# Modulation strips of a two-layer diffusion step: their matmuls beside the projections, one or two row chunks at a time or four

## The chip, the cores and the metric

The kernel runs on one core of a Trainium2 chip. The metric is the time of one execution on the device, in microseconds (us). The engines are PE (matrix products), DVE (vector operations), ACT (scalar operations, activations), POOL (GpSimd, here conv additions and memsets) and SP, which issues most DMA transfers. Each engine works through its own instructions in order and waits on semaphores for the others. SBUF is the memory on the chip that the engines read and write; PSUM, in banks, is where PE puts its results.

## The reference

Two layers work on 1152 tokens: 1024 latent tokens and 128 context tokens, each with 1024 features. What matters here is how the modulation enters:

```python
def ada_modulate(x, cond, norm_g, w_ada, b_ada):
    m = jax.nn.silu(cond) @ w_ada + b_ada
    shift, scale, gate = jnp.split(m, 3, axis=-1)
    h = rms_norm(x, norm_g) * (1.0 + scale[:, None, :]) + shift[:, None, :]
    return h, gate[:, None, :]
```

`cond` is one row for the context and one for the latent tokens, so `silu(cond) @ w_ada` is a product of 2 rows by a matrix of 1024 x 3072 for each layer. Layer 0 then projects `h` into the parts a, b, ga, q, k, v and gb. `a * sigmoid(b)` goes through a depthwise convolution of width 31, a layer norm and a SiLU, and is gated by `silu(ga)`; q, k and v go through an attention over a clamped 8 x 16 neighbourhood and all context keys, gated by `silu(gb)`. Both halves are concatenated and multiplied by `w_out`. Layer 1 projects its `h` into u and g, pools u over windows of 2, 4, 8 and 16 tokens, and multiplies by its own `w_out`. Each layer's result is multiplied by its gate and added to its input. The outputs are both streams after both layers, and the context keys and values of layer 0.

## The kernel before

**Tiling.** Tokens stand in three groups of 384. Matrices of float32 are split into a high and a low part, and a product is the sum of three matmuls of such parts. A chain of 24 matmuls (8 row blocks of 128, three products each) fills one PSUM bank: in L230 with 384 tokens as columns, for a, b, ga, gb and the projections of layer 1; in L237 with 128 tokens by 256 features, for v, q and k, where two chains share a bank, 48 matmuls in a row.

**Stages.** The rows of shift and scale of layer 0 come first, from the `wada` tiles. Then come items of work, one for each piece of `w_in_0`: `p_ab` for c = 0 to 3 (a and b of one quarter of the conv features each, three token groups g, two chains for each), `p_v` twice, `p_qk` four times, then gb and ga, the attention, the output of layer 0, and layer 1. The stretch of `p_ab`, `p_v` and the start of `p_qk` is 75 to 240 us in the profile.

**The strips.** What else of the modulation is needed, the gate of layer 0 and shift, scale and gate of layer 1, is computed beside these items, in three strips (`ada_strips`, called in `ada_rest`): for layer 0 four pieces of 256 columns, for layer 1 twice four pieces of 384. A strip has eight row chunks. Each chunk is one transfer (`wad`, 512 KB or 768 KB) by `dma_later` (L264, on SP's queue) into one of six slots `ADS`, and four matmuls (L360) with 2 columns of the two conditions as weights; the four go to the rows 0, 32, 64 and 96 of the bank through `tile_position`. Each such matmul of float32 is two records in the profile, so a chunk is eight. The bank (`tp`, of which there are two) is summed over the eight chunks.

**What follows a strip.** `fin` of the first strip is `ada_gate`: rows of the bias come by DMA (`gb`, L411), DVE adds and scales (L412, L413), and the result goes to memory (`gsc`, L414). `fin` of the others is `ada_cols`: POOL sets a tile `adr` to zero (L382) and DVE copies four pairs of rows into it (L384). It returns `ada_turn`, which is the strip's turn: three transposes on PE (L390) and additions on DVE (L278, L279). For the last strip the gate is formed as well.

**Who sets the order.** Steps stand in the queue `adq`, nine for a strip: eight chunks and the turn. `ada_steps(n)` takes n of them. It is called behind the chains of each token group in `p_ab` (two steps, one for c = 0), behind each pair of token blocks in `p_v` (one step), and before the first item of `p_qk`, where all that is left is taken. Between them `bg` advances streams of work in the background: the convolution, where for a tap ACT multiplies (L551) and POOL adds (L553) or DVE does both (L564). The first chains and the attention are put in order by hand; elsewhere the framework's scheduler puts each engine's instructions in order, from its own estimate of times, so that an edit of one step can move others. Of the last `qk` step DVE multiplies by `rstd` (L729), which POOL computes (L113, L114).

Of the kernel before, what the change touches and what calls it, by code (L numbers as in the profile page):

```python
# [46 lines left out]
def _body(tc, nc, A, O, const, wp, arena, tmpp, smp, psp):  # L47
# [7 lines left out]
    def slot(i, dtype=F32, name="s"):  # L55
        return arena.tile([P, SLOT], dtype, tag=f"S{i}", bufs=1, name=nm(name))
# [4 lines left out]
    def tmp(name="t"):  # L61
        return tmpp.tile([P, 512], F32, tag="t", name=nm(name))
# [22 lines left out]
    for w in (2, 4, 8, 16):  # L85
        t = const.tile([P, w], F32, name=f"corr{w}")
# [259 lines left out]
    adq = deque()  # L346

    def ada_strips(l, col, n, fin):

        st = {}  # L350

        def step(k):
            w = slot(ADS[st_i[0] % len(ADS)], name="wad")[:, : 4 * n]
            st_i[0] += 1
            dma_later(w, A[f"w_ada_{l}"][k * P : (k + 1) * P, col : col + 4 * n])
            if k == 0:
                st["b"] = bank("tp")
            for q in range(4):
                r = 32 * q
                te.matmul(  # L360
                    st["b"][r : r + 2, :n], sc[:, k, :], w[:, q * n : (q + 1) * n],
                    start=(k == 0), stop=(k == 7), tile_position=(0, r),
                )
            if k == 7:
                st["then"] = fin(st["b"])

        for k in range(8):
            adq.append(lambda k=k: step(k))
        adq.append(lambda: st["then"] and st["then"]())

    st_i = [0]

    def ada_steps(n=None):
        while adq and n != 0:
            adq.popleft()()
            n = None if n is None else n - 1

    def ada_cols(l, b, c0):

# [37 lines left out]
    def ada_rest():  # L417
        def fin11(b):
            then = ada_cols(1, b, 12)
            ada_gate(1, b, G, 1, P)  # L420
            return then

        ada_strips(0, 2 * D, 256, lambda b: ada_gate(0, b, 256, 0, 0))
        ada_strips(1, 0, G, lambda b: ada_cols(1, b, 0))
        ada_strips(1, 4 * G, G, fin11)

    def load_gates(l):
        gt = {}
# [217 lines left out]
    def p_ab(c):  # L646
        def glu(c, g, pa_, pb_):
            if g == 0:
                ut[c] = slot(US[c], name="u")[:, :UW] if c < 3 else gr[:, :UW]
                gp.memset(ut[c][:, 0:15], 0.0)  # L650
                gp.memset(ut[c][:, 1039:1054], 0.0)
                gp.memset(ut[c][:, 1182:1197], 0.0)
            th = tmp("th")
            se.activation(th[:, :G], pb_[:, :G], AF.Tanh, scale=0.5)
            for a, n, d in ((0, G, 15 + g * G),) if g < 2 else ((0, 256, 15 + 768), (256, P, 1054)):
                ve.scalar_tensor_tensor(ut[c][:, d : d + n], th[:, a : a + n], 1.0, pa_[:, a : a + n], ALU.add, ALU.mult)
            ready[c] = g + 1

        def chains(x, g, W):
            pa_, pb_ = bank("mm"), bank("mm")  # L660
            chain_ws(pa_[:, :G], W, 0, h0, g)
            chain_ws(pb_[:, :G], W, P, h0, g)
            glu(x, g, pa_, pb_)

        def fn(W):
            if c == 0:
                E = mybir.EngineType
                with tc.manual_schedule(engines={E.PE, E.Activation, E.DVE}):
                    bs = first_chains()
                units.update({x: [first_w[x, 0], first_w[x, 1]] for x in range(2)})  # L670
                W = units[0]
                late_vectors()
                for x, g in bs:
                    glu(x, g, *bs[x, g])
                make_h0(2)
                chains(1, 1, units[1])
            for g in range(2 if c < 2 else 0, 3):
                chains(c, g, W)
                bg(6000)
                ada_steps(2 if c else 1)  # L680
        return fn

    def p_v(vb):
        def fn(W):
            for t in range(0, 9, 2):
                b = bank("mm")
                n = min(2, 9 - t)
                for i in range(n):
                    chain_tok(b[:, i * 256 : (i + 1) * 256], W, h0, t + i)
                if t == 8:  # L690
                    se.copy(VP[:, vb * 256 : (vb + 1) * 256], b[:, :256])
                else:
                    s = tmp("vst")
                    se.copy(s, b)  # L694
                    se.dma_start(
                        vs[t * P : (t + 2) * P, vb * 256 : (vb + 1) * 256].rearrange("(a p) c -> p a c", p=P),
                        s.rearrange("p (a c) -> p a c", a=2),
                    )
                bg(4500)
                ada_steps(1)  # L700
            if vb == 1:
                se.dma_start(O[3][0], VP.rearrange("p (h d) -> p h d", d=64))
        return fn
# [4 lines left out]

    def p_qk(pr):
        def fn(W):  # L710
            if pr == 0:
                ada_steps()
            if pr == 2:
                bg_until(lambda: len(done) >= 1)
            for t in range(0, 9, 2):
                n = min(2, 9 - t)
# [757 lines left out]
```

## Time and profile before

| | |
|---|---|
| time, median of 3 runs | 974.99 us (974.53 to 975.31) |
| the profiled execution | 977.55 us, span 975.8 us |
| PE busy | 948.4 us, 97% of the span |
| DVE busy | 601.9 us, 62% |
| ACT busy | 404.4 us, 41% |
| POOL busy | 369.8 us, 38% |
| granted clock of PE, mean | 0.996 |

The span reaches from the first to the last instruction of the profiled execution; its own time is that of the whole execution. Busy shares are means over all stages. Records of PE overlap, since a matmul begins before the one ahead of it has ended; distances between starts are what counts. The granted clock is a share of PE's full clock.

### The profile page before, as it was taken

What the parts mean: (1) busy time and instruction counts of PE and PEld (TensorE: products, weight loads), DVE (VectorE), ACT (ScalarE), POOL (GpSimd) and SP (SyncE); (2) the same over time, 40 slices, a digit from 0 to 9 for tenths busy, and PEclk for the clock granted to TensorE, in tenths of its full rate; (3) what the DMA queues carried; (4) which work ended last, traced back from release to release, by engine and by line L of the source; (5) the groups of instructions that cost most, each with busy time, mean ns of one, the idle gap of its engine ahead of it and who ended that gap; (6) DMA issues with size and microseconds to landing.
All of it is one profiled execution on the core that took longest, in us unless ns stands there. A gap on an engine that the chain in (4) does not pass through costs nothing.

```text
span 975.8 us, 16659 instructions
## 1 busy us (share of the span) xinstructions
PE 948.4 (97%) x6388; PEld 866.3 (89%) x6388; DVE 601.9 (62%) x1243; ACT 404.4 (41%) x815; POOL 369.8 (38%) x485
## 2 busy tenths in 40 slices
PE   4999999899999999999999999999999999999998
PEld 2899888789999999987887888889999999998887
DVE  3658999989783444457778447666335554585332
ACT  4374676765411244238887223344222122231010
POOL 2354899889943201024456145430000000004231
PEclk9999999899999999999999999999999999999999
DMA  9946955525111111135335412251111111133211
GB/s 311 304 190 153 348 183 184 173 88 185 46 47 46 48 44 44 36 90 142 109 114 175 130 65 108 84 165 44 34 43 33 44 44 55 65 112 129 105 65 66
DMA packets 87531, 108.54 MB, mean 111 GB/s; under 512 B 10700, under 2 KB 73036, under 8 KB 87339
## 3 DMA queue, kind: packets, MB, share of 16 engines
q1 hardware_dynamic: 82539, 95.93, 30.9%
q0 software_dynamic: 2576, 9.18, 2.4%
q10 hardware_dynamic: 2336, 2.36, 0.7%
q8 instruction: 50, 0.82, 0.3%
q14 instruction: 30, 0.25, 0.1%
HBM read 94.64 MB, written 21.57 MB: 119 GB/s over the span
## 4 chain that ended last, share of the span: by engine, by line
PE 82%; POOL 5%; DVE 3%; DMA 3%; ACT 2%; issue 2%; SPq 1%; DVEq 0%; ACTq 0%; POOLq 0%
PE mm L230 33%; PE mm L237 15%; PE mm L1210 10%; PE mm L1203 10%; POOL zc L553 5%; PE cv L985 3%; PE tp L976 2%; PE mm L952 2%; PE mm L1373 2%; DVE cv L564 1%; DMA x<-in_x_sample 1%; DMA raw<-in_w_in 1%; PE tp L443 1%; SPq L212 1%; PE cv L230 1%
## 5 line engine op out<-in xcount | busy, mean ns | idle before, releaser
L230 PE MATMUL mm<-h,whi 128*128 128x384 f32 x1504 | 389.5, 339 | 1.0 <-POOL h L450 0.4
L230 PEld LDWEIGHTS mm<-h,whi 128*128 128x128 f32 x1504 | 271.6, 189 | 6.8 <-issue 2.0
L230 PE MATMUL mm<-h,wlo 128*128 128x384 f32 x752 | 252.8, 337 | 0.0
L553 POOL TENSOR_TENSOR zc<-zc,gr 128x384 f32<-128x384 f32 x138 | 148.5, 1078 | 32.7 <-ACT gr L551 24.5
L237 PE MATMUL mm<-whi,h 128*128 128x256 f32 x864 | 160.6, 287 | 0.0
L237 PEld LDWEIGHTS mm<-whi,h 128*128 128x128 f32 x864 | 137.4, 194 | 6.5 <-ACT vst L694 3.3
L230 PEld LDWEIGHTS mm<-h,wlo 128*128 128x128 f32 x752 | 141.9, 189 | 0.0
L237 PE MATMUL mm<-wlo,h 128*128 128x256 f32 x432 | 123.3, 285 | 0.0
L187 DVE TENSOR_TENSOR wlo<-raw,whi 128x1024 fp32r<-128x1024 f32 (+1 forms) x56 | 67.5, 1206 | 53.3 <-ACT whi L186 53.2
L564 DVE SCALAR_TENSOR_TENSOR cv<-u,convw,cv 128x384 f32<-128x384 f32 (+1 forms) x208 | 95.8, 514 | 1.3
L1210 PE MATMUL mm<-wrh,zs 128*128 128x512 f32 x288 | 92.4, 392 | 0.2 <-POOL wrh L1179 0.2
L1203 PE MATMUL mm<-whi,zs 128*128 128x512 f32 (+1 forms) x304 | 92.5, 379 | 0.0
L186 ACT CAST whi<-raw 128x1024 fp32r<-128x1024 f32 (+1 forms) x56 | 56.9, 1018 | 69.8 <-PE mm L230 25.9
L237 PEld LDWEIGHTS mm<-wlo,h 128*128 128x128 f32 x432 | 84.0, 194 | 0.0
L1217 POOL TENSOR_TENSOR y<-y,og 128x512 f32<-128x512 f32 x34 | 48.6, 1430 | 83.4 <-DVE og L1215 80.3
L551 ACT ACTIVATE gr<-u,convw 128x384 f32<-128x384 f32 (+2 forms) x128 | 64.3, 531 | 30.5 <-POOL zc L553 29.8
L970 POOL TENSOR_SCALAR p<-p,st 128x512 f32<-128x512 f32 x64 | 48.6, 773 | 47.6 <-DVE st L968 31.7
L1203 PEld LDWEIGHTS mm<-whi,zs 128*128 128x128 f32 x304 | 56.0, 188 | 10.6 <-ACT whi L186 0.2
L1210 PEld LDWEIGHTS mm<-wrh,zs 128*128 128x128 f32 x288 | 53.9, 188 | 11.8 <-POOL wrh L1179 0.6
L1215 DVE TENSOR_TENSOR og<-mm,gr 128x512 f32<-128x512 f32 x34 | 23.3, 687 | 59.3 <-PE mm L1210 35.0
L533 ACT ACTIVATE th<-mm 128x384 f32<-128x384 f32 x48 | 23.5, 489 | 81.7 <-PE mm L230 81.5
L1203 PE MATMUL mm<-wlo,zs 128*128 128x512 f32 (+1 forms) x152 | 57.2, 378 | 0.0
(215 smaller groups left out, 1393.2 us busy)
## 6 DMA issues: line engine op xcount, KB each, us to landing
raw<-in_w_in SPq DMA_DIRECT2D x28, 512.0 KB
wad<-in_w_ada SPq DMA_DIRECT2D x16, 768.0 KB
wada<-in_w_ada SPq DMA_DIRECT2D x16, 512.0 KB
raw<-in_w_in SPq DMA_DIRECT2D x32, 256.0 KB
raw<-in_w_out SPq DMA_DIRECT2D x16, 512.0 KB
y0scr<-y POOLq DMA_DIRECT2D x9, 512.0 KB, 3.2
y<-y0scr SPq DMA_DIRECT2D x9, 512.0 KB
x<-in_x_sample SPq DMA_DIRECT2D x8, 512.0 KB
```

Source lines behind the costliest of these rows:

```text
L186: se.copy(hi[:, :n], raw[:, :n])
L187: ve.tensor_tensor(lo[:, :n], raw[:, :n], f(hi[:, :n]), ALU.subtract)
L230: te.matmul(out, wsl(units, a, k, c0, P), hsl(hs, b, k, g), start=(k == 0 and i == 0), stop=(k == nk - 1 and i == 2))
L237: te.matmul(out, hsl(hs, p, k, g, a, P), wsl(units, q, k, 0, 256), start=(k == 0 and i == 0), stop=(k == 7 and i == 2))
L551: se.activation(pr[:, o : o + n], src, AF.Copy, scale=w)
L553: gp.tensor_tensor(z, z, pr, ALU.add)
L564: ve.scalar_tensor_tensor(zp if k == 30 else acc, src, convw[:, c, k : k + 1], zp if k == NPTS[c] else acc, ALU.mult, ALU.add)
L970: gp.tensor_scalar(ps[i][:, e, :], ps[i][:, e, :], st[:, 4 + e : 5 + e], 0.0, ALU.mult, ALU.add)
L985: te.matmul(ob[64 * e : 64 * e + 64, i * P : (i + 1) * P], vw[j0 + i][x][:, 64 * e : 64 * e + 64], pts[i][:, e, n * P : (n + 1) * P], star ...
L1203: te.matmul(b[:, c0 : c0 + n], zs[p][:, k, :], WL[k // 2][q][:, k % 2, c0 : c0 + n], start=(k == 0 and i == 0), stop=(k == 7 and i == 2))
L1210: te.matmul(b, zs[p][:, k, :], WR[q][k // 3][:, k % 3, :], start=(k == 0 and i == 0), stop=(k == 7 and i == 2))
L1217: gp.tensor_tensor(yv, yv, t, ALU.add)
```

## The change

An entry of the queue is now a list of steps, called a portion here: four chunks of a strip. The turn of a strip is no entry of its own; it stands at the head of the next strip's first portion (`owed_turn`), and that of the last strip in a portion alone. `ada_steps` takes one portion, and is called at seven named places: behind the token groups (c, g) = (1, 2), (2, 1), (3, 0) and (3, 2) of `p_ab`, and behind the blocks (vb, t) = (0, 4), (1, 0) and (1, 6) of `p_v`. The call in `p_qk` is gone. The instructions are the same on each engine, in another order.

```diff
--- before.py
+++ after.py
@@ -364,16 +364,17 @@
             if k == 7:
                 st["then"] = fin(st["b"])
 
-        for k in range(8):
-            adq.append(lambda k=k: step(k))
-        adq.append(lambda: st["then"] and st["then"]())
-
-    st_i = [0]
-
-    def ada_steps(n=None):
-        while adq and n != 0:
-            adq.popleft()()
-            n = None if n is None else n - 1
+
+        then, owed_turn[:] = list(owed_turn), [lambda: st["then"] and st["then"]()]
+        adq.append(then + [lambda k=k: step(k) for k in range(4)])
+        adq.append([lambda k=k: step(k) for k in range(4, 8)])
+
+    st_i, owed_turn = [0], []
+
+    def ada_steps(n=1):
+        for _ in range(min(n, len(adq))):
+            for step in adq.popleft():
+                step()
 
     def ada_cols(l, b, c0):
 
@@ -423,6 +424,7 @@
         ada_strips(0, 2 * D, 256, lambda b: ada_gate(0, b, 256, 0, 0))
         ada_strips(1, 0, G, lambda b: ada_cols(1, b, 0))
         ada_strips(1, 4 * G, G, fin11)
+        adq.append(list(owed_turn))
 
     def load_gates(l):
         gt = {}
@@ -677,7 +679,8 @@
             for g in range(2 if c < 2 else 0, 3):
                 chains(c, g, W)
                 bg(6000)
-                ada_steps(2 if c else 1)
+                if (c, g) in ((1, 2), (2, 1), (3, 0), (3, 2)):
+                    ada_steps()
         return fn
 
     def p_v(vb):
@@ -697,7 +700,8 @@
                         s.rearrange("p (a c) -> p a c", a=2),
                     )
                 bg(4500)
-                ada_steps(1)
+                if (vb, t) in ((0, 4), (1, 0), (1, 6)):
+                    ada_steps()
             if vb == 1:
                 se.dma_start(O[3][0], VP.rearrange("p (h d) -> p h d", d=64))
         return fn
@@ -708,8 +712,6 @@
 
     def p_qk(pr):
         def fn(W):
-            if pr == 0:
-                ada_steps()
             if pr == 2:
                 bg_until(lambda: len(done) >= 1)
             for t in range(0, 9, 2):
```

On PE, in the order of before, the 24 chunks stand in 18 groups between chains: in the first strip groups of a quarter of a chunk, three quarters, 2, 2, 2 and 1; in the second 2, 2, 2, 1 and 1; in the third six of 1 and one of 2. Of the changed kernel they stand in six groups of four. The next rows are PE's order of before at the first group of two (`tp_996` is the bank of the first strip, `mm` banks are those of the chains, a row with x4 is one chunk).

```order
L230 MATMUL mm_1030<-h_756,whi_568 128x384
L230 MATMUL mm_1030<-h_755,wlo_569 128x384
L360 MATMUL tp_996<-wad_1095,sc 2x256 x4
L360 MATMUL tp_996<-wad_1101,sc 2x256 x4
L230 MATMUL mm_1119<-h_249,whi_1007 128x384
L230 MATMUL mm_1119<-h_250,whi_1007 128x384
```

In the changed kernel the same place has four chunks, and no chunk stands earlier (`tp_1090` is now the bank of the first strip).

```order
L230 MATMUL mm_1023<-h_756,whi_568 128x384
L230 MATMUL mm_1023<-h_755,wlo_569 128x384
L360 MATMUL tp_1090<-wad_1088,sc 2x256 x4
L360 MATMUL tp_1090<-wad_1095,sc 2x256 x4
L360 MATMUL tp_1090<-wad_1101,sc 2x256 x4
L360 MATMUL tp_1090<-wad_1107,sc 2x256 x4
L230 MATMUL mm_1125<-h_249,whi_1000 128x384
L230 MATMUL mm_1125<-h_250,whi_1000 128x384
```

What moved: the first chunk's four matmuls, which were parted over two earlier places, and the fourth chunk, which came a token group later.

The second place is the order on DVE around the copies into `adr` of the second strip (its bank is `tp_1519` in both). Before, they are rows 253 to 256 of DVE's order; the products that form the conv input (L656, `gr`) stand some thirty rows ahead.

```order
L564 SCALAR_TENSOR_TENSOR cv_2084<-u_1169,convw,cv_2084 128x384
L564 SCALAR_TENSOR_TENSOR cv_1893<-u_743,convw,cv_1893 128x128
L564 SCALAR_TENSOR_TENSOR cv_2084<-u_1169,convw,cv_2084 128x384
L384 COPY adr_1927<-tp_1519 2x384
L564 SCALAR_TENSOR_TENSOR cv_1893<-u_743,convw,cv_1893 128x256
L384 COPY adr_1927<-tp_1519 2x384 x3
L564 SCALAR_TENSOR_TENSOR cv_2084<-u_1169,convw,cv_2084 128x384
```

In the changed kernel they stand one tap behind those products, now L658 (the copies are L385, the taps L566).

```order
L658 SCALAR_TENSOR_TENSOR gr_73<-th_1679,mm_1629 128x256
L658 SCALAR_TENSOR_TENSOR gr_73<-th_1679,mm_1629 128x128
L566 SCALAR_TENSOR_TENSOR cv_1375<-u_736,convw,cv_1375 128x128
L385 COPY adr_1746<-tp_1519 2x384 x4
L566 SCALAR_TENSOR_TENSOR zc_970<-u_743,convw,cv_1698 128x384
L566 SCALAR_TENSOR_TENSOR cv_1375<-u_736,convw,cv_1375 128x256
```

What moved: four copies, ahead of some thirty taps. The memset of `adr` on POOL stands eight conv additions earlier too, and the first `rstd` of q and k behind 117 conv additions in place of 119.

The third place is SP's queue while the tables of the relative bias (`texp`) are written; `raw` are pieces of `w_in_0`. Before:

```order
L804 DMA texp<-tbias 384x256 x6
L264 DMA wad_1399<-in_w_ada 128x1024
L212 DMA raw_1115<-in_w_in 128x4x256
L264 DMA wad_1517<-in_w_ada 128x1536
L804 DMA texp<-tbias 384x256 x2
L212 DMA raw_1117<-in_w_in 128x4x256
L264 DMA wad_1524<-in_w_ada 128x1536
L264 DMA wad_1617<-in_w_ada 128x1536
```

In the changed kernel, where wad_1291 and wad_1297 are the last two chunks of the second portion:

```order
L806 DMA texp<-tbias 384x256 x7
L264 DMA wad_1291<-in_w_ada 128x1024
L212 DMA raw_1121<-in_w_in 128x4x256
L264 DMA wad_1297<-in_w_ada 128x1024
L264 DMA wad_1517<-in_w_ada 128x1536
L264 DMA wad_1524<-in_w_ada 128x1536
L806 DMA texp<-tbias 384x256
L212 DMA raw_1123<-in_w_in 128x4x256
```

What moved: seven of the eight `texp` transfers now stand ahead of the second portion's last two chunks; before, a chunk (wad_1399) stood behind the sixth, and the first wide one (wad_1517) ahead of the last two.

## Rows read from the trace of the kernel before

**Rows 1.** The head of the page and its first part: the span, and of each engine its busy time, share of the span and instructions.

```profile
span 975.8 us, 16659 instructions
...
PE 948.4 (97%) x6388; PEld 866.3 (89%) x6388; DVE 601.9 (62%) x1243; ACT 404.4 (41%) x815; POOL 369.8 (38%) x485
```

**Rows 2.** The waits of PE between 75 and 320 us: the engine, operation and line that waited, for whom, us in total, times, longest. It is the view's only line.

```profile
PE tp L390 <- POOL zc L553: 3.2, 1, 3.2
```

**Rows 3.** The windows view: the stretch in us, its length, then busy time (and instructions) of PE, of PE's weight loads, of DVE, ACT and POOL, the granted clock of PE, the share of time that the DMA engines were busy, and GB/s.

```profile
100.00:125.00 25.00, 25.00 (x168) 22.49 (x167) 24.34 (x52) 16.73 (x30) 21.31 (x21) 1.00 0.93 337
...
170.00:175.00 5.00, 1.85 (x14) 1.68 (x13) 4.91 (x12) 3.38 (x6) 4.69 (x5) 0.81 0.17 57
175.00:180.00 5.00, 5.00 (x25) 5.00 (x25) 4.97 (x16) 3.36 (x6) 4.61 (x6) 0.51 0.64 210
```

**Rows 4.** PE's timeline around matmuls of L360 on chunks of 256 columns, between the chains of L230 (one line is a run of like matmuls: start, length, line, operands, forms, count). Left out between 80.98 and 81.77 is a group of two records (a quarter of a chunk), between 121.00 and 121.81 one of eight (a chunk).

```profile
80.98 0.34 PE L230 MATMUL mm<-h,whi 128*128 128x384 f32 x1
...
81.77 0.44 PE L230 MATMUL mm<-h,whi 128*128 128x384 f32 x1
...
90.08 0.51 PE L230 MATMUL mm<-h,whi 128*128 128x384 f32 x2
...
92.50 0.34 PE L230 MATMUL mm<-h,wlo 128*128 128x384 f32 x1
92.77 1.04 PE L360 MATMUL tp<-wad,sc 128*2 128x256 f32 x16
93.75 0.44 PE L230 MATMUL mm<-h,whi 128*128 128x384 f32 x1
...
102.27 1.04 PE L360 MATMUL tp<-wad,sc 128*2 128x256 f32 x16
...
121.00 0.34 PE L230 MATMUL mm<-h,wlo 128*128 128x384 f32 x1
...
121.81 0.62 PE L230 MATMUL mm<-h,whi 128*128 128x384 f32 x2
```

**Rows 5.** PE's timeline, matmuls of L360 on chunks of 384 columns: a group of two chunks (16 records) between chains of L230 and the next such group, then a group of one chunk (8 records) between chains of L237 and the next.

```profile
130.34 1.47 PE L360 MATMUL tp<-wad,sc 128*2 128x384 f32 x16
...
140.26 1.47 PE L360 MATMUL tp<-wad,sc 128*2 128x384 f32 x16
...
193.37 0.83 PE L360 MATMUL tp<-wad,sc 128*2 128x384 f32 x8
...
200.08 0.83 PE L360 MATMUL tp<-wad,sc 128*2 128x384 f32 x8
```

**Rows 6.** PE's timeline from the end of one chain of L237 over the first transposes of L390 to the end of the next chain.

```profile
170.71 0.28 PE L237 MATMUL mm<-whi,h 128*128 128x256 f32 x1
174.14 0.72 PE L390 MATMUL tp<-ident,adr 98*128 98x98 f32 x3 [3.15 <-POOL zc L553]
174.56 0.56 PE L237 MATMUL mm<-whi,h 128*128 128x256 f32 x1
...
175.13 0.63 PE L237 MATMUL mm<-whi,h 128*128 128x256 f32 x2
...
179.61 0.55 PE L237 MATMUL mm<-whi,h 128*128 128x256 f32 x2
180.00 0.28 PE L237 MATMUL mm<-wlo,h 128*128 128x256 f32 x1
...
182.63 0.28 PE L237 MATMUL mm<-whi,h 128*128 128x256 f32 x1
```

**Rows 7.** PE's timeline around the second transposes of L390, which start at 224.31 us.

```profile
224.07 0.40 PE L237 MATMUL mm<-whi,h 128*128 128x256 f32 x2
...
224.71 0.40 PE L237 MATMUL mm<-whi,h 128*128 128x256 f32 x2
```

**Rows 8.** The timeline of POOL (first line) and of DVE between 146 and 175 us: the memset of the tile adr, the products of L656, conv taps and the copies of L384.

```profile
147.20 0.42 POOL L382 MEMSET adr<- 98x384 f32 x1
...
158.29 0.60 DVE L656 SCALAR_TENSOR_TENSOR gr<-th,mm 128x256 f32<-128x256 f32 x2
...
168.85 2.57 DVE L564 SCALAR_TENSOR_TENSOR cv<-u,convw,cv 128x128 f32<-128x128 f32 x6
171.33 0.54 DVE L384 COPY adr<-tp 2x384 f32<-2x384 f32 x1
...
172.30 1.70 DVE L384 COPY adr<-tp 2x384 f32<-2x384 f32 x3
```

**Rows 9.** The timeline of SP's DMA queue between 97 and 118 us (start and length are those of the issuing), and the page's line on a transfer of 512 KB, with us from issue to landing at its end.

```profile
97.31 3.83 SPq L804 DMA_DIRECT2D texp<-tbias  x6
...
107.98 5.29 SPq L264 DMA_DIRECT2D wad<-in_w_ada  x4
114.13 3.76 SPq L411 DMA_DIRECT2D gb<-in_b_ada  x4
...
y0scr<-y POOLq DMA_DIRECT2D x9, 512.0 KB, 3.2
```

**Rows 10.** DVE's timeline at the first q and k block, PE's timeline at 242 us, and of the lines view of POOL between 100 and 230 us the line of its conv additions (busy us, mean ns, idle us before them and what ended most of it).

```profile
235.79 0.75 DVE L729 TENSOR_TENSOR qk<-mm,rstd 128x256 f32<-128x256 f32 x2
...
241.97 0.40 PE L237 MATMUL mm<-whi,h 128*128 128x256 f32 x2
...
L553 POOL TENSOR_TENSOR zc<-zc,gr 128x384 f32<-128x384 f32 x105 | 114.1, 1089 | 15.9 <-ACT gr L551 9.0
```

## The prediction

> **What bounds the kernel now.** I read the page first: PE is busy for 948.4 of a span of 975.8 us, no other engine for more than 62% [rows 1]. So the sum can only be made of two things: matmul time that PE no longer spends, and moments in which PE stands still. Next I asked for PE's waits in the stretch that the change touches, 75 to 320 us. There is one, of 3.2 us, before the transposes of L390 [rows 2]. The windows come third [rows 3]: the granted clock is 0.81 from 170 to 175 us and 0.51 from 175 to 180, the lower of its two levels (1.2 of 2.4 GHz), right behind that wait, and 1.00 in the stretch before; and DVE is busy nearly all of the time from 100 us on (24.34 of 25 us), so whatever is queued behind work on DVE comes late. Last I read PE's timeline around the strips' matmuls [rows 4, 5] and around that wait [rows 6].
>
> **The switch into and out of a strip.** A chain's matmuls of 384 columns follow each other every 0.173 us (90.08 to 92.50 us, 14 of them). Two chunks of 256 columns stand between 92.77 and 93.75 us, and from one such group to the next is 9.50 us, where 48 chain matmuls alone take 8.32: a group of two costs 1.18 us [rows 4]. From the last chain matmul before that group to the first behind it is 1.25 us, 1.08 over the pitch; so 0.10 of the 1.18 lies in the matmuls right behind. With the same 0.10, the single chunk at 121 us costs 0.81 - 0.17 + 0.10 = 0.74 us, and the quarter of a chunk at 81 us 0.72 [rows 4]. Two chunks less one give 0.44 us for a chunk and leave 0.30 for a group, whatever is in it; that the quarter costs as much as a chunk says the same. For 384 columns the two-chunk period is 9.92 us, a cost of 1.60, and the one-chunk period between chains of 48 matmuls at 0.1195 us (5.74; the pitch from 180.00 to 182.63, 22 of them [rows 6]) is 6.71, a cost of 0.97, say 0.95 [rows 5]: 0.65 a chunk and 0.30 a group again.
>
> Before, by the order on PE: strip one has groups of a quarter, three quarters, 2, 2, 2 and 1 chunks, 0.72 + 0.74 + 3 x 1.18 + 0.74 = 5.7 us; strip two has 2, 2, 2, 1, 1, 3 x 1.60 + 2 x 0.95 = 6.7; strip three six single ones and a pair, 6 x 0.95 + 1.60 = 7.3. Together 19.7 us. After: two groups of four narrow chunks, 2 x (0.30 + 4 x 0.44) = 4.1, and four of wide ones, 4 x (0.30 + 4 x 0.65) = 11.6: 15.7 us. Term one is **-4.0 us**, all of it on PE and so on the path. Its bounds are 0 (if the 0.30 came from something else than the switch) and -5.0 (if the 0.10 behind each group went twice).
>
> The Trainium skill (TensorEngine Tiling (Array Packing), Tiling Modes, Key Properties) says that a change of tiling mode drains TensorE, and its page TensorE: Matmul & The Clock Gate (Part 2, what each phase is for) puts a drain at about 128 cycles. Two drains a group would by that be 0.11 us, an estimate, and twelve groups fewer 1.3 us in place of 3.6, so a sum smaller by 2.3 us. The trace shows 0.30 for a group and agrees with the rule, not with the figure alone.
>
> **The transposes of L390.** PE ends its chain at 170.71, begins the transposes at 174.14 and the next chain at 174.56; its matmuls then stand 0.213 us apart (175.13 to 179.61, 21 of them) and only from 180.00 on 0.12 [rows 6]. From 170.71 to 182.63 are 48 chain matmuls: 11.92 us in place of 5.74. The second set of transposes, which waits for nothing, adds 0.28 (224.07 to 224.71 less three matmuls) [rows 7]. So the wait costs 11.92 - 5.74 - 0.28 = **5.9 us**, of which only 3.2 are seen as a wait; the rest is the half clock. The view names POOL as releaser, but POOL's memset was done at 147.6. What came last are DVE's four copies: the first at 171.33, the other three from 172.30 to 174.0, queued behind conv taps (L564) that DVE had been given since its gate product at 158.29 [rows 8].
>
> After, the order on DVE has the four copies one tap behind that gate product, so at about 159.2 us, and at 0.57 us each (1.70 for three [rows 8]) done by 161.6. Portion four, which they read, ends on PE near 151, and PE comes to the transposes at 170.9 less what strips one and two save by then, 5.7 + 6.7 - 4.1 - 5.8 = 2.5, so at 168.4. The margin is 6.8 us, and nothing else is waited for, the memset moving eight taps forward. Term two is **-5.9 us**, bounds 0 (copies late after all) and -6.2. No other queue pays: the copies come sooner on DVE by taps that nobody waits for there, at 2.3 us.
>
> **The chunks' transfers.** A portion needs four chunks landed, where a group before needed two, and four of six slots. Portion two is the tight one: PE comes to it at 111.77 - 1.76 = 110.0 (1.76 is what strip one has saved by then) and wants its last chunk 1.5 us later, after the switch and three chunks at 0.44: 111.5. By the order on SP that transfer now stands behind seven texp transfers, another chunk and a weight piece. Those began at 97.31 [rows 9]; 7 x 0.39 + 2 x 0.52 + 0.26 = 4.1 MB at the 337 GB/s of that stretch [rows 3] take 12.0 us, so they are through at 109.4 without an allowance for latency, 112.6 with 3.2 us for it, which is what a transfer of 512 KB takes from issue to landing at the row of y0scr [rows 9]. The worst bound is the next line of SP in the trace, 114.13 [rows 9]. The wait is 0 to 2.6 us; I take **+0.5**, near the early side since chunks of before at the same place were never waited for [rows 2]. Behind this wait stands all of PE's queue. The bias rows of the first gate are queued earlier on DVE; if DVE waits for them, taps are late, not PE. The later portions ask for slots that the order frees a whole item before; I take nothing for them.
>
> **What is late next.** From 220 us on PE comes 8.6 us earlier to the q and k blocks, whose PSUM banks DVE empties. At 242.09 (the second matmul of the row at 241.97) PE writes a bank that DVE freed at 236.54: 5.55 us of margin [rows 10]. Without any help 3.1 us of the gain would be waited out there. Help comes: POOL, on whose rstd that DVE instruction depends, has two taps fewer ahead of it in the new order (2 x 1.09 us), and 9.0 us of POOL's idle time in 100 to 230 us is waiting for ACT [rows 10], some 4 of it after 180 us behind ACT's copies of results that PE gave late. So the path moves by 2.2 to 6 us and the loss is 0 to 3.1; I take **+0.8**, as both helps are likely.
>
> **The sum.** -4.0 - 5.9 + 0.5 + 0.8 = -8.6 us. The profiled execution took 977.55, which is 1.75 around its span, and 2.56 over the median of the runs; the same sum is taken off the median: 974.99 - 8.6 = **966.4 us**. Without the two losses it is 965.1, with both at their ends (2.6 + 3.1) 970.8.
>
> **Rivals.**
> - DVE and POOL become the bound in the q and k blocks: the full 3.1 us are given back there, perhaps in two items. For it: DVE's share in rows 3, the margin in rows 10, both engines' work unchanged. Against it: the taps end by about 270 us, and margins grow. Gain 4 to 6.5 us, 968.5 to 971.
> - The change does half of what it says. Either the groups cost by columns alone and only the wait goes, 974.99 - 5.9 + 1.3 = 970.4; or DVE's copies still come late, and only the switches are saved, about 971. The orders speak against the second, the quarter chunk of rows 4 against the first.
> - The portions wait for their last chunk. If a chunk lands 3 us after PE wants it, PE stands still and its clock is halved, as in rows 6, for 5.9 us a time. One such wait leaves a gain of 4.0 + 5.9 - 5.9 = 4.0 us, 971. Two, at portions two and three, cost 11.8 against 9.9: slower, 976.9. It decides from 3 us of lateness; for it speak 337 GB/s with the DMA engines 0.93 busy [rows 3] and four chunks of six slots; against it that portion three's margin is over 4 us by the SP order. The Trainium skill (TensorE: Matmul & The Clock Gate, HAM oscillation) describes this: compute shorter than a transfer's wait restarts cold at each tile. Rows 6 agree for one wait; none here shows it for a transfer.
>
> **How the numbers follow.** This kernel's runs tell 0.2%, about 2 us, from no change. Forecast 0.6, within 964.5 to 968.5 by its own terms; DVE and POOL 0.15; half of the effect 0.1; one late portion 0.09; two 0.06. So faster 0.9, and within 0.2% (a late portion with other losses) 0.05, slower 0.05. The range goes from 964.0 (no loss, and the 5.0 end of term one) to 972.0, past one late portion, and leaves out two.
>
> **What would show it.** In the changed profile: six groups of L360, each of 32 matmul records, at 2.06 us (narrow) and 2.90 (wide); no wait before the transposes (now L391), and a granted clock of 1.00 from 165 to 180 us; DVE's copies done by 162; no wait of PE between 75 and 320 longer than 1 us. A wait of PE for a transfer at L360 near 110 us, or one for DVE's product at L731 near 233, would be the losses; a clock below 1.00 near 110 would make the prediction wrong.

## The result and the profile after

In four runs each the changed kernel took 968.15 us (967.81 to 968.54) and the kernel before 975.15 us (974.53 to 976.22): a ratio of 0.9927 with a 95% interval of 0.9910 to 0.9944, 7.0 us faster. In two later jobs the ratio was 0.9937 (0.9923 to 0.9950) and 0.9948 (0.9935 to 0.9960), 6.5 and 5.4 us. The forecast was 966.4 us, a gain of 8.6, in a range of 964.0 to 972.0.

The two profiled executions lie further apart than the medians: 977.55 and 967.94 us, 9.6 us. The head of the page of the changed kernel, to be read against [rows 1]:

```profile
span 966.2 us, 16658 instructions
...
PE 941.5 (97%) x6388; PEld 864.2 (89%) x6388; DVE 603.1 (62%) x1243; ACT 403.7 (42%) x815; POOL 368.9 (38%) x485
```

The same matmuls, and 6.9 us less in which PE was busy: matmuls at the low clock count as longer ones, and a group of L360 holds the chain behind it up while PE counts as busy. The waits of PE between 75 and 320 us, the view of [rows 2], have one line again, but another one:

```profile
PE mm L237 <- DVE qk L731: 1.2, 1, 1.2
```

The windows answer to [rows 3] (the columns are those given there): the clock is full where it had been 0.81 and 0.51.

```profile
165.00:170.00 5.00, 5.00 (x53) 3.79 (x56) 5.00 (x16) 3.22 (x7) 4.73 (x5) 1.00 0.93 288
170.00:175.00 5.00, 5.00 (x49) 4.14 (x38) 5.00 (x13) 3.37 (x6) 4.65 (x5) 1.00 0.95 347
175.00:180.00 5.00, 5.00 (x44) 5.00 (x43) 5.00 (x17) 3.13 (x6) 4.76 (x6) 1.00 0.56 212
```

PE's timeline at the second and third portion, and over the transposes, which answers to [rows 4 to 6]:

```profile
109.34 0.34 PE L230 MATMUL mm<-h,wlo 128*128 128x384 f32 x1
109.61 1.91 PE L360 MATMUL tp<-wad,sc 128*2 128x256 f32 x32
111.45 0.62 PE L230 MATMUL mm<-h,whi 128*128 128x384 f32 x2
...
128.05 0.34 PE L230 MATMUL mm<-h,wlo 128*128 128x384 f32 x1
128.32 2.76 PE L360 MATMUL tp<-wad,sc 128*2 128x384 f32 x32
131.01 0.62 PE L230 MATMUL mm<-h,whi 128*128 128x384 f32 x2
...
167.81 0.28 PE L237 MATMUL mm<-whi,h 128*128 128x256 f32 x1
167.93 0.42 PE L391 MATMUL tp<-ident,adr 98*128 98x98 f32 x3
168.28 2.76 PE L360 MATMUL tp<-wad,sc 128*2 128x384 f32 x32
```

A narrow portion costs 111.45 - 109.34, less the pitch of 0.17, plus the 0.10 behind it: 2.04 us. A wide one, 2.96 by the same count, costs 2.89. The transposes start 0.12 us after the last chain matmul, which is a pitch: nothing is waited for. The copies that they read, on DVE:

```profile
158.65 0.61 DVE L658 SCALAR_TENSOR_TENSOR gr<-th,mm 128x256 f32<-128x256 f32 x2
159.18 0.34 DVE L566 SCALAR_TENSOR_TENSOR cv<-u,convw,cv 128x128 f32<-128x128 f32 x1
159.43 2.25 DVE L385 COPY adr<-tp 2x384 f32<-2x384 f32 x4
```

They end at 161.7, 6.2 us ahead of PE. So the steps of the prediction show: the wait is gone, and there are six groups at the price that was forecast. What does not fit is the size, 8.6 against 7.0 us, while the two profiles show even 9.6.

### The profile page after: what moved, and what is told of

Same layout as the page of the kernel before. It is cut to its first block, busy times and chain, and to the rows that moved or that the text cites. A ratio compares the mean times of both kernels' runs of the same rounds, so it can differ in the third digit from the quotient of the medians.

```text
span 966.2 us, 16658 instructions
## 1 busy us (share of the span) xinstructions
PE 941.5 (97%) x6388; PEld 864.2 (89%) x6388; DVE 603.1 (62%) x1243; ACT 403.7 (42%) x815; POOL 368.9 (38%) x485
## 4 chain that ended last, share of the span: by engine, by line
PE 77%; POOL 8%; DVE 5%; ACT 3%; DMA 3%; issue 2%; SPq 1%; ACTq 0%; DVEq 0%; POOLq 0%
PE mm L230 35%; PE mm L1212 10%; PE mm L1205 10%; PE mm L237 8%; POOL zc L555 8%; PE cv L987 3%; PE tp L978 2%; DVE cv L566 2%; PE mm L954 2%; PE mm L1375 2%; PE tp L445 1%; PE cv L230 1%; ACT gr L553 1%; DMA raw<-in_w_out 1%; DVE wlo L187 1%
## 5 line engine op out<-in xcount | busy, mean ns | idle before, releaser
L230 PE MATMUL mm<-h,whi 128*128 128x384 f32 x1504 | 388.5, 338 | 1.0 <-DVE h L451 0.4
L230 PEld LDWEIGHTS mm<-h,whi 128*128 128x128 f32 x1504 | 271.4, 189 | 4.4 <-issue 1.3
L230 PE MATMUL mm<-h,wlo 128*128 128x384 f32 x752 | 252.6, 337 | 0.0
L237 PE MATMUL mm<-whi,h 128*128 128x256 f32 x864 | 156.8, 284 | 1.2 <-DVE qk L731 1.2
L230 PEld LDWEIGHTS mm<-h,wlo 128*128 128x128 f32 x752 | 141.9, 189 | 0.0
L237 PEld LDWEIGHTS mm<-whi,h 128*128 128x128 f32 x864 | 135.1, 192 | 3.3 <-issue 1.4
L237 PE MATMUL mm<-wlo,h 128*128 128x256 f32 x432 | 122.2, 283 | 0.0
L566 DVE SCALAR_TENSOR_TENSOR cv<-u,convw,cv 128x384 f32<-128x384 f32 (+2 forms) x208 | 95.0, 515 | 0.8
L186 ACT CAST whi<-raw 128x1024 fp32r<-128x1024 f32 (+1 forms) x56 | 56.9, 1018 | 64.8 <-PE mm L230 25.4
L237 PEld LDWEIGHTS mm<-wlo,h 128*128 128x128 f32 x432 | 82.9, 192 | 0.0
```

Source lines behind the costliest of these rows:

```text
L186: se.copy(hi[:, :n], raw[:, :n])
L230: te.matmul(out, wsl(units, a, k, c0, P), hsl(hs, b, k, g), start=(k == 0 and i == 0), stop=(k == nk - 1 and i == 2))
L237: te.matmul(out, hsl(hs, p, k, g, a, P), wsl(units, q, k, 0, 256), start=(k == 0 and i == 0), stop=(k == 7 and i == 2))
L566: ve.scalar_tensor_tensor(zp if k == 30 else acc, src, convw[:, c, k : k + 1], zp if k == NPTS[c] else acc, ALU.mult, ALU.add)
```

## The experiments

A measure for all of them: from the start of the last `cv` matmul of L230 (near 63 us, ahead of the strips) to the start of the last L237 matmul with `wlo` (end of q and k). The lines view by source gives both; of one execution of the changed kernel (the third profile, below), minimum, median and longest ns, then first and last start:

```profile
L230 PE MATMUL cv<-h,wlo x16: 334/334/339, 31.1 to 62.7; 128*128 128x384 f32 x16
...
L237 PE MATMUL mm<-wlo,h x432: 278/283/283, 150.5 to 312.2; 128*128 128x256 f32 x144
```

312.2 - 62.7 = 249.5 us. All profiles by that measure, but for the two of kernels that leave the modulation out; groups are runs of L360 between other matmuls:

| kernel | groups | stretch, us | waits of PE in it |
|---|---|---|---|
| before, first profile | 18 | 259.1 | 3.2 at L390, clock falls |
| before, second | 18 | 253.9 | 0.5 at L390 |
| before, third | 18 | 255.8 | 2.4 at L390 |
| turn later, first and second | 18 | 253.2, 254.1 | none; 0.7 at the second turn |
| portions of one, first and second | 24 | 254.8, 254.7 | none |
| portions of two | 13 | 251.8 | none |
| changed, first to third | 6 | 250.6, 250.7, 249.5 | 1.2, 1.2 at q and k; none |
| changed, fifth portion earlier | 7 | 254.7 | 3.3 at L391, clock falls |

**The kernel before again.** No edit.

> The kernel before, unchanged, for a second profile. The two profiles differ by 9.6 us in span (975.8 and 966.2) and the medians by 7.0. Theory: the first profiled execution was a long one, and a second has a span near 973.5, with the wait at L390 and the stretch of low clock behind it shorter by 1 to 2.5 us than 3.2 and 6.8 us. Rival: what is missing lies elsewhere (start or end of the execution), then the wait is 3.2 us again and the span differs before 75 or behind 320 us. Second rival: every profile of before is at 975.8 and a profiled execution is as such longer.

Its time was 972.76 us, its span 971.0, 4.8 less than in the first profile. PE's timeline:

```profile
170.97 0.28 PE L237 MATMUL mm<-whi,h 128*128 128x256 f32 x1
171.71 0.44 PE L390 MATMUL tp<-ident,adr 98*128 98x98 f32 x3 [0.46 <-DVE adr L384]
171.93 0.36 PE L237 MATMUL mm<-whi,h 128*128 128x256 f32 x1
```

The wait is 0.46 us here, the view names DVE's copies as releaser, and the clock does not fall. Compared one by one, DVE's instructions in the first profile are 2.6 us later at 96 us and still 2.4 later at the copies, while those of PE are 0.3 us earlier, until L390. What came late stands in ACT's timeline, the cast (L186) of a piece of `w_in_0`, first in the first profile, then in the second (the bracket is the idle time ahead and its releaser):

```profile
95.33 1.05 ACT L186 CAST whi<-raw 128x1024 fp32r<-128x1024 f32 x1 [4.51 <-DMA raw<-in_w_in]
```

```profile
92.71 1.05 ACT L186 CAST whi<-raw 128x1024 fp32r<-128x1024 f32 x1 [1.63 <-DMA raw<-in_w_in]
```

One weight piece was there 2.6 us later, and DVE waited for its part of it. From 97 to 170 us DVE is idle for only 2.6 us of 73, most of it in waits for ACT and POOL, which are late by the same delay; so it kept the delay until the copies. The delay shows on SP's queue already, where the issue of two pieces ahead of `texp` takes longer, first in the first profile, then in the second:

```profile
91.54 3.20 SPq L212 DMA_DIRECT2D raw<-in_w_in  x2
```

```profile
90.87 1.29 SPq L212 DMA_DIRECT2D raw<-in_w_in  x2
```

The theory held in kind: the 5.9 us that the prediction priced are those of such an execution. Its numbers were short: a span near 973.5 and a wait shorter by 1 to 2.5 us had been expected, and it was 971.0 and 2.7. The rivals fell: the stretch alone is 5.2 us shorter, and the span is not at 975.8 again.

**And a third time**, in another job.

> The kernel before once more, for a third profile. Theory: the wait at L390 follows what DVE lost near 95 us to a late weight piece. With ACT's cast of that piece at 92.7 us the wait is about 0.5 us, at 95.3 it is 3.2, and in between it is the cast's start less 92.2; the clock falls only with the long wait. Rival: the wait varies by itself, by PE or by POOL, with the cast at the same time.

974.3 us, span 972.5. ACT's cast started at 94.05, between the two, and PE's timeline has

```profile
170.23 0.28 PE L237 MATMUL mm<-whi,h 128*128 128x256 f32 x1
172.89 0.44 PE L390 MATMUL tp<-ident,adr 98*128 98x98 f32 x3 [2.38 <-POOL zc L553]
173.11 0.36 PE L237 MATMUL mm<-whi,h 128*128 128x256 f32 x1
```

so a wait in between, without a fall of the clock. The expected 1.85 us (94.05 - 92.2) was short, because PE itself came 0.7 us earlier than in the second profile. Over the three, DVE's product ahead of the copies starts at 158.29, 155.85 and 157.06 us, and the wait is 3.15, 0.46 and 2.38: the wait follows DVE's delay and PE's own arrival. DVE's last copy ends 0.14, 0.16 and 0.15 us ahead of the transposes in the three, whatever releaser the view names. The issue of the two pieces on SP's queue took 2.79 us in this profile, again in between. Why it takes longer in some executions was not tried.

**The turn moved alone.** The kernel before, a strip's turn queued behind the next strip's second chunk (the line for the last strip is left out here):

```diff
         for k in range(8):
             adq.append(lambda k=k: step(k))
-        adq.append(lambda: st["then"] and st["then"]())
+            if k == 1:
+                adq.extend(owed_turn)
+                owed_turn.clear()
+        owed_turn.append(lambda: st["then"] and st["then"]())
```

> The kernel before with the turn of a strip two steps later, behind the first two chunks of the next strip; the chunks stay in 18 groups of one or two. PE then comes to the transposes some 76 chain matmuls (9 us) later, and DVE's copies stay where they were in its order. Theory: the wait of 3.2 us and the half clock behind it go, 5.9 us by the profile, and at most 1 us is given back at q and k: 969 to 970.5 us, with no wait at L390 in the profile and a clock of 1.00 from 165 to 180 us. Rival one: only the visible 3.2 us go, 972. Rival two: the switches are what the change saves and the stall counts for nothing, 975.

971.95 us against 972.81 for before, a ratio of 0.9985 (0.9976 to 0.9994): 0.9 us. The wait at the first turn is gone and the clock is 1.00 throughout, but in that job before itself had a median 2.3 us lower than in the first comparison, so there was less to gain. The forecast of 969 to 970.5 had been counted from 975, and that the rival's 972 is met says as little. The 11 times lie within 1.2 us, the 27 of before within 4.0. By the stretch it is 253.2 us, and so, if nothing else differs, the stall had cost 5.9, 0.7 and 2.6 us in the three profiles of before.

**Groups, counted apart.** The changed kernel with portions of one chunk, called at more places, in `p_ab` also between two chains (the calls are left out here): `adq.append((then if k == 0 else []) + [lambda k=k: step(k)])`.

> The changed kernel with portions of one chunk, called at 24 places: 24 groups in place of six, the transposes at the same place in PE's order. Theory: each group costs 0.30 us beside its chunks, so 18 x 0.30 = 5.4 us more than the changed kernel, 973.5, with a cost of a narrow single chunk of 0.74 in the profile. Rival one: a group costs 0.11 us (two drains by the figure that the Trainium skill gives), 970.1. Rival two: the groups cost nothing and the columns alone count, 968.2.

972.90 us, a ratio to before of 0.9996 (0.9987 to 1.0005). The changed kernel was not in that job, so the 973.5 was met only in absolute time. The stretch says it better: 254.8 us, 5.3 over the 249.5 of the changed kernel without a wait, where 18 groups at 0.30 make 5.4. From the chain matmul ahead of a single narrow chunk to the one behind it are 0.81 us (83.43 to 84.24), a cost of 0.74 as expected.

**The turn opened too early.** The changed kernel, fifth portion at the first blocks of `p_v`:

```diff
-                if (vb, t) in ((0, 4), (1, 0), (1, 6)):
+                if (vb, t) in ((0, 0), (1, 0), (1, 6)):
```

> The changed kernel with the fifth portion, which the turn opens, called two pairs of token blocks earlier. PE then comes to the transposes near 156.7 us, while DVE's copies end at 161.7 as in the changed kernel. Theory: PE waits 5 us there, its granted clock falls to half for some 7 us, and the loss is 5 + 2.5 to 3, less up to 1.2 us that the wait at q and k had cost: 974.5 to 976. Rival: the clock does not fall and only the wait counts, 972 to 973. Second rival: the copies are not what the transposes wait for, 968.

973.10 us, a ratio of 1.0002 (0.9993 to 1.0011): no faster than before (the changed kernel itself was not in that job). The timelines of DVE and of PE, and the windows of 5 us:

```profile
158.29 2.25 DVE L385 COPY adr<-tp 2x384 f32<-2x384 f32 x4
```

```profile
157.06 0.28 PE L237 MATMUL mm<-whi,h 128*128 128x256 f32 x1
160.68 0.72 PE L391 MATMUL tp<-ident,adr 98*128 98x98 f32 x3 [3.34 <-DVE adr L385]
161.33 3.45 PE L360 MATMUL tp<-wad,sc 128*2 128x384 f32 x24
```

```profile
155.00:160.00 5.00, 2.33 (x20) 2.13 (x18) 4.96 (x11) 3.10 (x6) 4.76 (x4) 1.00 0.67 203
160.00:165.00 5.00, 4.32 (x29) 1.39 (x30) 4.97 (x15) 3.86 (x8) 4.61 (x6) 0.66 0.98 351
```

The copies ended at 160.5, 1.2 us sooner than expected, so the wait was 3.3 and not 5. The clock falls to 0.66 in the window behind, and the stretch is 5.2 us longer than that of the changed kernel without a wait (254.7 - 249.5): the stall of before, made in the changed kernel by its place. Some 0.3 of the 5.2 is another cost: the order parts this portion into groups of three chunks and one, so that there are seven groups. The time of 974.5 to 976 was too high because the wait was shorter, and the stretch of half clock behind it too. By the windows it is (0.34 x 5) / 0.5 = 3.4 us, where [rows 3] give (0.19 x 5 + 0.49 x 5) / 0.5 = 6.8 for the first profile of before, and some 7 had been expected.

**The changed kernel again.** No edit.

> The changed kernel, unchanged, for a second profile and for times beside the kernel before in more rounds. In the second profile of the kernel before the wait at L390 was 0.5 us without a fall of the clock, in the first 3.2 us with one; in the first every instruction of DVE from 96 us on was 2.6 us later, behind a weight piece that landed late. Theory: the stall's 5.9 us are there in some executions of before only, the typical one has about 0.5, so the gain is 4.0 + 0.5 less 0 to 1.2 at q and k, 3.3 to 4.5 us or 0.35 to 0.45%, with a longer tail on the side of before; the executions of the changed kernel lie within 1.5 us of each other. Rival: the 7.0 us (0.7%) of the first comparison stand.

968.64 us (967.46 to 969.01) against 975.16 (972.07 to 978.12): 6.5 us. The theory's 3.3 to 4.5 us were too few; the rival's 7.0 lies within the interval (4.9 to 7.5 us). Before had its stalls in that job, as the granted clock on record for each execution says: 0.998 or less in 6 of 13, which took 976.2 us in the mean, against 973.8 for the other seven. In the job with 972.81 it is one of 27, and none of 21 in the last job; of the changed kernel none of 15. So the stall with a fall of the clock is frequent in one job and rare or absent in others, and the gain is larger where it is frequent. The times of before are spread over 6 us here, where those of the changed kernel lie within 1.6. The wait at q and k was 1.2 us again. DVE's and PE's timelines of the first profile show it, two products of one block with a conv tap between them:

```profile
234.61 0.42 DVE L731 TENSOR_TENSOR qk<-mm,rstd 128x256 f32<-128x256 f32 x1 [0.19 <-POOL rstd L114]
234.95 0.61 DVE L566 SCALAR_TENSOR_TENSOR zc<-gr,convw,cv 128x384 f32<-128x384 f32 x1
235.47 0.42 DVE L731 TENSOR_TENSOR qk<-mm,rstd 128x256 f32<-128x256 f32 x1
```

```profile
236.03 0.36 PE L237 MATMUL mm<-whi,h 128*128 128x256 f32 x1 [1.18 <-DVE qk L731]
```

**Portions of two.** `for k in range(0, 8, 2): adq.append((then if k == 0 else []) + [lambda k=k: step(k), lambda k=k: step(k + 1)])`, called at 13 places and not at seven (left out here).

> The changed kernel with portions of two chunks at twice the places: 13 groups (the scheduler puts one matmul of the first chunk ahead of the rest) in place of six, the transposes at the same place. Theory, 0.30 us a group: 7 x 0.30 = 2.1 us over the changed kernel, less up to 1.2 us of the wait at q and k which PE then no longer meets. Rival (0.11 us a group): 0.8 us over it, less the same, so no difference.

970.43 us, 1.8 over the changed kernel in the same job, with no wait at q and k; the theory had 0.9 to 2.1, the rival no difference. By the stretch 251.8 - 249.5 = 2.3 us for seven groups.

**What a group costs beside its chunks: the tile position?** The changed kernel with all four pieces on rows 0 and 1 (what reads the bank reads those rows; left out here):

```diff
-                    st["b"][r : r + 2, :n], sc[:, k, :], w[:, q * n : (q + 1) * n],
-                    start=(k == 0), stop=(k == 7), tile_position=(0, r),
+                    st["b"][0:2, :n], sc[:, k, :], w[:, q * n : (q + 1) * n],
+                    start=(k == 0 and q == 0), stop=(k == 7 and q == 3),
```

> The changed kernel with the strips' matmuls all on rows 0 and 1 of their bank and no tile position; the four pieces of a strip are summed over each other, so the gates, shifts and scales are left out in what they should be. Theory, the Trainium skill's rule that a change of tiling mode drains TensorE: the 0.27 us from the last chain matmul to the first of L360 and the late matmuls behind it go, the cost of a group beside its chunks falls from 0.30 to under 0.1. Rival: the 0.30 comes from the change of operands (from the split halves to whole float32, with weights of 2 columns), then it stays. In both the chunks themselves may get dearer, since four positions no longer work side by side: up to 4 x 0.43 = 1.7 us for a narrow chunk by the 8 matmuls of 256 columns in it. So the time is no measure here, only the starts in the timeline.

PE's timeline at the first portion:

```profile
90.67 0.34 PE L230 MATMUL mm<-h,wlo 128*128 128x384 f32 x1
90.94 7.07 PE L360 MATMUL tp<-wad,sc 128*2 128x256 f32 x32
97.94 0.62 PE L230 MATMUL mm<-h,whi 128*128 128x384 f32 x2
98.40 0.33 PE L230 MATMUL mm<-h,wlo 128*128 128x384 f32 x1
```

0.27 us ahead of the group and 0.46 for two matmuls behind it, 0.11 more than two pitches: as with the tile position. The theory fell. The 32 matmul records take 7.00 us in place of 1.84. The last of them alone:

```profile
97.63 0.38 PE L360 MATMUL tp<-wad,sc 128*2 128x256 f32 x1
```

The 31 steps from 90.94 to 97.63 are 0.216 us each, but from there to the chain's first matmul it is 0.31: 0.09 more. With the 0.10 ahead of the group (0.27 less the pitch of 0.17) and the 0.11 behind, these are the 0.30 of a group. The steps are even where one chunk ends and the next, with a transfer of its own, begins, so to depend on a new transfer is not what costs.

**Or the kind of operands?** The same, and the two operands of L360 (here L362) as split halves:

```diff
-                    st["b"][0:2, :n], sc[:, k, :], w[:, q * n : (q + 1) * n],
+                    st["b"][0:2, :n], scr[:, k, :], hsl(h0, 0, k, 0)[:, :n],
```

> As the run without tile position, but the strips' matmuls take operands of the split kind that the chains use (a piece of the normalized input in place of the row chunk, and the conditions in that kind); the modulation they should give is left out. Without the tile position the 0.27 us ahead of a group and the 0.11 behind it had stayed. Theory: they come from the change between whole float32 and split operands on PE; then the first matmul of L360 follows the chain's last after 0.17 us, its pitch, and the first two of the chain behind stand 0.17 apart. Rival: they come from the weights of 2 columns in place of 128, then 0.27 and 0.11 stay. The time is no measure here.

```profile
92.21 0.34 PE L230 MATMUL mm<-h,wlo 128*128 128x384 f32 x1
92.38 1.99 PE L362 MATMUL tp<-h,scr 128*2 128x256 f32 x16
94.20 0.51 PE L230 MATMUL mm<-h,whi 128*128 128x384 f32 x2
94.55 0.34 PE L230 MATMUL mm<-h,wlo 128*128 128x384 f32 x1
```

The group follows after 0.17 us, its 16 records fill the 1.82 us to the chain at 0.114 each, the last step included, and the two matmuls behind it take 0.35, a pitch each: none of the three parts is left. The weights have 2 columns still. So the extra time at both ends of a group comes with matmuls of whole float32, two records each, between those of split operands; both operands were changed at once. Operands of whole float32 alone do not do it: the transposes, one record each, follow a chain after a pitch (167.81 to 167.93 above), and `adr` and `ident` are float32.

**All three in one job**: the turn moved alone, the changed kernel, and 24 groups.

> The kernel before with the turn two steps later, once more, beside the changed kernel and 24 groups in one job. Theory: against before it gains what the stall costs in the mean of executions, 1 to 4 us (0.9 in the job with a median of before of 972.8, more where before is slower), and its executions lie closer together than those of before; the changed kernel is 12 x 0.30 = 3.6 us faster than this, less up to 1.2 us at q and k: 2.4 to 3.6. Rival: the stall's share is the same 0.9 us on every chip.

> The changed kernel beside the others. Theory: 2.4 to 3.6 us under the turn moved alone, 18 x 0.30 - 1.2 = 4.2 to 5.4 us under 24 groups, a wait of 1.2 us at q and k in the profile and no other. Rival (0.11 us a group): 1.3 and 2.0 us under them.

> 24 groups of one chunk beside the others. Theory: 6 x 0.30 = 1.8 us over the turn moved alone (18 groups), 4.2 to 5.4 over the changed kernel. Rival (0.11 us a group): 0.7 and 2.0 over them.

Before took 972.71 us, the turn moved alone 972.08 (ratio 0.9992, 0.9983 to 1.0001), the changed kernel 967.34 and 24 groups 972.84. The changed kernel is 5.5 us under 24 groups (4.2 to 5.4 had been expected) and 4.7 under the turn moved alone, above the 2.4 to 3.6: its profile had no wait at q and k this time, and that of the turn moved alone had 0.7 us at the second turn, which is the next to be late. So moving the turn alone does not end the waiting. Two expectations failed. The turn moved alone gained 0.6 us and not 1 to 4, in a job in which before had no fall of the clock, and its times lie 2.7 us apart, those of before 2.1. And 24 groups are only 0.8 us over it, where the theory had 1.8 and the rival of 0.11 us a group 0.7; against the changed kernel, 5.5 us to the rival's 2.0, that rival falls. The stretches without any wait give 249.5 us for 6 groups, 251.8 for 13, 253.2 for 18 and 254.7 for 24: 0.33, 0.31 and 0.29 us a group over six. The 13 and the 18 have one chunk parted in two, which by the 0.44 of a chunk is paid twice; less that it is 0.27, 0.27 and 0.29. That chunk and the wait at the second turn, 0.44 + 0.7 us, are about the 1.0 that is missing between 24 groups and the turn moved alone.

## Why the prediction was right, and where it was off

**The switches.** Term one said 0.30 us a group and 4.0 us for twelve fewer. The groups cost 2.04 and 2.89 us where 2.06 and 2.90 were forecast, and the stretch without waits is 253.2 - 249.5 = 3.7 us shorter. Right in size. Its reason was left open as "the switch". The rule beside it is that a change of tiling mode drains TensorE (the Trainium skill, TensorEngine Tiling (Array Packing), Tiling Modes, Key Properties). The runs do not bear it out as the cause: without a tile position the 0.27 and 0.11 us stayed, with split operands and the same 2 columns they went. In which mode the array ran in either, no profile shows, so a mode that depends on the kind of operands is not excluded. Rows and rule had only seemed to agree. One argument was none: that a quarter of a chunk costs as much as a chunk does not say that the cost is the group's. The four positions work side by side (1.84 us, on one position 7.00), so a quarter takes as long as the whole. The 0.30 comes from two chunks less one, and the experiments with 13, 18 and 24 groups bear it out.

**The stall.** The mechanism is shown: DVE's copies behind conv taps, PE waiting, a half clock behind it, gone with the copies 6.2 us early (6.8 were forecast), and brought back in the changed kernel by opening the turn sooner. The size was off, and this is the step that was mis-sized: "So the wait costs 5.9 us", taken from one execution and then "off the median". The profiled execution was 2.56 us over the median, and the stall is what made it long; in two other profiles it cost 0.7 and 2.6 us. Less the 2.56 it is 3.3, an estimate that puts all of the excess down to the stall. The mean of the three, (5.9 + 0.7 + 2.6) / 3 = 3.1, is near it, and that is all that three executions can say. In the last job, where the clock of before fell in no execution, 1.7 of 5.4 us are left for the stall and all else.

**The transfers.** +0.5 was taken, 0 came. PE was at portion two at 109.61 (110.0 forecast). The SP queue of the changed kernel issued all of it some 3 us sooner than the sum, which begins at 97.31, allowed for:

```profile
94.08 5.29 SPq L806 DMA_DIRECT2D texp<-tbias  x7
99.47 0.78 SPq L264 DMA_DIRECT2D wad<-in_w_ada  x1
100.35 0.49 SPq L212 DMA_DIRECT2D raw<-in_w_in  x1
100.93 2.92 SPq L264 DMA_DIRECT2D wad<-in_w_ada  x3
```

In its other two profiles `texp` starts at 94.94 and 92.62, and in the second and third of before at 94.73 and 96.05: the 97.31 was late by the same delay as DVE, so this term too was taken from an unusual execution. The sum also had the weight piece at 0.26 MB, and it is one of 512 KB in the view of the transfers. The rival of late chunks did not occur in any of the three profiles.

**What is late next.** +0.8 was taken; it was 1.2, 1.2 and 0 us, at the second block of q and k, not at the first that the prediction looked at. There DVE's product waits for POOL's `rstd` and is parted by a tap. Whether less work on DVE or POOL would end it was not tried.

**The sum.** With terms as measured or estimated: -3.7 for the groups, -3.3 for the stall in the first comparison, 0 for the transfers, 0 to +1.2 at q and k. That is 5.8 to 7.0 us, against 7.0, 6.5 and 5.4 in the three comparisons. That the first two alone make 7.0 is in part luck. The profile of the changed kernel in that comparison lost 1.2 at q and k, and a share of the gain stood in no term: from the end of the stretch to the end of the span the three profiles of before take 653.3, 653.5 and 653.8 us, those of the changed kernel 652.6, 652.4 and 652.7. Of this 1.0 us, PE's wait for POOL's `wrh` in the last product (L1210) is 0.2 to 0.8 before and at most 0.2 after; why it is shorter stays open.

## What to carry to other kernels

Before a wait of the profiled execution is priced, ask whether that execution is a usual one: if it lies above the median by more than runs differ, the wait may be what put it there, and only the rest of it can be expected from the median. A wait that hangs on an engine with hardly any idle time inherits the delays that this engine met earlier, here 75 us before. Putting the two ends further apart takes away the wait in the late executions as well as in the usual ones; moved by too little, the wait can come back at the next place, as at the second turn. Small matmuls of another operand kind between long chains cost a fixed price at each change (some 0.3 us a group here), so they are better bundled, as far as buffers let their inputs arrive in time.

## What had not been expected of the hardware

- A group of matmuls of whole float32 among those of split operands on PE cost 0.10 us ahead of it (0.27 in place of 0.17), 0.09 from its last record to the chain (0.31 in place of 0.216) and 0.11 in the two matmuls behind; spreading over four positions of the array and weights of 2 columns added none that these rows show.
- Four positions side by side in the array took 1.84 us for 32 matmul records of 256 columns, one position alone 7.00: 3.8 times.
- PE's clock went to its lower level (1.2 of 2.4 GHz) after waits of 3.2 and 3.3 us, and stayed at 2.4 GHz after waits of 2.4, 1.2 and 0.5 us. Behind the first two it stayed low for 6.8 and 3.4 us. A wait of 3.2 us thus cost 5.9, one of 2.4 us 2.6.
- The same kernel's median was 975.15, 972.81, 975.16 and 972.71 us in four jobs, a spread of 2.5 us; the changed kernel's was 968.15, 968.64 and 967.34. In the one of these jobs with a fall of the clock in 6 of 13 executions, these took 2.4 us longer than the others.
